# Gate steps in fours behind whole tree levels and in the attention; meta-token products over 128 rows; values turned two stages later

## The chip, the core and the metric

The kernel runs on one core of a Trainium2 chip. The metric is the device time of one execution in microseconds; of several runs the median is given. Inputs are float32. Matrix products of weights are made in three products of fp32r halves (high and low parts); the small products of the attention and of the recurrences are plain float32, which TensorE runs in two passes, so that one product is two MATMUL instructions in the trace.

## What is computed

Two blocks follow each other over 512 tokens of width 1024. The change lies in the mixer of the second block, which runs two layers over 528 tokens (16 meta tokens ahead of the 512):

```python
for l in range(DEPTH_2):                                   # two layers
    u = rms_norm_2(h, ln_mix[l])
    (aq, ak, av, bq, bk, bv, cq, ck, cv, dq, dzf, dzb, di, dg, gz) = split_in(u @ w_in[l])
    y_a = windowed_sink_attention(aq, ak, av, attn_sink[l], bias_a)
    y_b = axial_rope_attention(rms_norm_2(bq, ...), rms_norm_2(bk, ...), bv, row, col, key_ok)
    y_c = differential_attention(cq, ck, cv, lam, bias_c, key_ok, diff_subnorm[l], lam_init)
    y_d = hgrn2_bidirectional(dq, dzf, dzb, di, dg, lb_all[0, l], lb_all[1, l], valid, hgrn_out_norm[l])
    gate = jax.nn.sigmoid(gz)                              # four gates of width 1024 per token
    merged = gate[:, :, 0] * (y_a @ w_branch[l, 0])        # ... + gate n * (branch n @ w_branch[l, n])
    h = h + merged @ w_out[l]
    u = rms_norm_2(h, ln_ffn[l])
    h = h + (jax.nn.silu(u @ w_ffn_gate[l]) * (u @ w_ffn_up[l])) @ w_ffn_down[l]
```

The gates `gz` are the largest part of the projection: 4096 columns, and nothing before the merge needs them.

## The kernel before

Activations lie with features on the partitions, 528 columns (16 meta tokens, then four tiles of 128). A weight block is 128 output features by 1024 inputs. `wget` (L310) loads it on SyncE's queue into `raw` (three buffers), casts the high half `wh` on ScalarE and forms the low half `wl` on VectorE; `mm3` (L326) then makes three products for each of eight slices of the inputs.

`mixer2(l)` (L1457) runs for l = 0 and 1. In layer 0 all 528 tokens are queries, in two pieces of 264 columns; in layer 1 only the 512, in one piece. Its parts in order:

- **The gates as filler.** `gates()` (L1472) is a generator over 32 weight blocks. One call of `next` is a *gate step*: one slice of one block, that is six products `pgz` of 264 columns in layer 0 and three of 512 in layer 1. Eight steps are a block, 256 steps a layer. `self.fill(n)` (L356) takes n steps wherever the code calls it, and `self.fill(256)` after the attention takes what is left.
- **The recurrence** (`hgrn`, L1265). After ten weight blocks there are two *trees* (m = 0, 1), each for two heads, which lie on partitions 0 to 63 and 64 to 127. A tree has nine levels H = 1 to 256 and one more product of the same kind. A level forms `KH` and `QH` from `q`, the gates and running products (`QH` and the updates of `df` on VectorE, `KH` and the updates of `Sx` and `Px` on GpSimd). `put` (L1331) then multiplies them: four blocks b of 128 tokens, each for both heads, which is a *group* of four 64-row MATMUL instructions (`pA`). The result is copied into `AD` under a mask (L1348, VectorE; the first level by ScalarE). In layer 0 some levels have 16x16 products of the meta tokens as well (`pAm`). Level 128 and level 256 are copied to `A1`, `A2`, `A3` by ScalarE, the product with the meta keys to `AM` (16 rows). Then for each head x and token tile t five output products go into `pod`: four over 128 rows and one over the 16 rows of `AM` and `Vd[4]`.
- **The projections** of the other three branches: twelve weight blocks in `staged(12, first, sums, roped)`. In `staged`, stage j works on block i - j, so `sums` is one block behind `first`, and `roped` two. Blocks 3, 7 and 11 are values: `values` turns them with `turnV`, five transposes (`pvt`) that ScalarE copies into `V`. Queries and keys go to DRAM (`qkd`).
- **The third branch** (differential attention, four heads with 5 or 4 query tiles): `prepare` reads keys and queries back (`T<-qkd`, two buffers; cast to `A` on ScalarE, corrected on GpSimd), then `scores` (`pS`), `combine`, `turn` (`ptp`, transposed into `PT` for 512 keys and `PT4` for the 16 meta keys) and `product` (`po`, five products a tile, the last over 16 rows).
- **The first two branches** in `attention` (L763): eight units, each with `att_max` (`pS`), `att_exp` (`pm`, `pT`) and `att_pv` (`po`).
- **The merge** (`pbr`) and the output product (`pwo`).

The program's order on an engine is not that of the code alone: a scheduler places an instruction earlier where its operands are ready and buffers are free. Each engine then runs its list strictly in order. PSUM has eight banks: four for projections and gates (`acc`), four for everything else (`mx`).

## Time and profile before

| | |
|---|---|
| median of 3 runs | 3375.02 us (3368.74 to 3382.93) |
| profiled execution | 3379.54 us |
| its span, first to last instruction | 3377.7 us |
| mean granted TensorE clock | 0.964 of full speed |
| TensorE (PE) busy | 3262.8 us, 97% |
| VectorE (DVE) busy | 1722.3 us, 51% |
| ScalarE (ACT) busy | 1144.0 us, 34% |
| GpSimd (POOL) busy | 468.5 us, 14% |

The profiled execution's own time is 1.8 us above its span. Busy time counts an engine from the start of an instruction to its end; matmuls overlap in the array, so neighbouring starts tell more of TensorE than its busy share. In a timeline row stand the start and the time of a merged group of instructions, engine, line, operation, output<-inputs, shape and count, and in brackets the idle time before it with what ended it. Lines L241, L247, L266 and L269 are helpers that record every product, elementwise operation, activation and copy, so tiles are told apart by names. The first tree of layer 0 lies at 1317 to 1386 us of the span, its second at 1418 to 1483; those of layer 1 at 2415 to 2469 and 2498 to 2558.

### The profile page before, as it was taken

How to read it: one execution, taken by the hardware profiler on the slowest of the kernel's cores; microseconds unless marked ns; L12 is line 12 of the kernel's file. 1: busy time of each engine (PE TensorE's matmuls, PEld its weight loads, DVE VectorE, ACT ScalarE, POOL GpSimd, SP SyncE). 2: the span in 40 equal slices, each digit the busy share in tenths (PEclk: the TensorE clock that was granted, in tenths of full speed). 3: DMA queues.
4: the chain of work that ended last, by engine and by line, in shares of the span. 5: the costliest groups of instructions: out<-in, count | busy, mean ns of one | idle time of the engine just before them, and what ended most of it. 6: DMA issues, size and time to landing. Idle time of an engine off the chain costs nothing. (4 is left out here: it accounts for less than half of the span.)

```text
span 3377.7 us, 47662 instructions
## 1 busy us (share of the span) xinstructions
PE 3262.8 (97%) x18886; PEld 2770.6 (82%) x18886; DVE 1722.3 (51%) x3632; ACT 1144.0 (34%) x1958; POOL 468.5 (14%) x575
## 2 busy tenths in 40 slices
PE   8999999899999999998999999999999899999998
PEld 6778778877888889888888999999767788788886
DVE  4443378553544445654763744433665474654433
ACT  4222343366322333222642232222222453232221
POOL 1010010412000013322120300000331221400000
PEclk9999989898999999998997999999999898899999
DMA  4333213322323233233332522233223342522322
GB/s 128 104 107 115 87 63 107 99 88 69 94 94 94 94 100 110 77 102 106 108 115 68 157 88 91 93 99 116 88 84 103 117 130 88 162 90 97 93 93 77
DMA packets 121271, 337.26 MB, mean 100 GB/s; under 512 B 28853, under 2 KB 29248, under 8 KB 121048
## 3 DMA queue, kind: packets, MB, share of 16 engines
q1 hardware_dynamic: 87656, 267.95, 24.8%
q0 software_dynamic: 21712, 54.51, 5.2%
q10 hardware_dynamic: 11680, 11.76, 1.1%
q8 instruction: 148, 2.42, 0.3%
q14 instruction: 75, 0.61, 0.1%
HBM read 298.42 MB, written 39.56 MB: 100 GB/s over the span
## 5 line engine op out<-in xcount | busy, mean ns | idle before, releaser
L269 ACT CAST wh<-raw 128x1024 fp32r<-128x1024 f32 (+1 forms) x448 | 463.7, 1035 | 1571.2 <-issue 766.1
L247 DVE TENSOR_TENSOR wl<-raw,wh 128x1024 fp32r<-128x1024 f32 (+1 forms) x448 | 560.9, 1252 | 412.3 <-ACT wh L269 410.3
L241 PE MATMUL pg<-xl,wh 128*128 128x512 f32 (+1 forms) x880 | 283.2, 354 | 12.7 <-DVE xl L259 12.7
L241 PE MATMUL pg<-xh,wh 128*128 128x512 f32 (+1 forms) x880 | 282.1, 353 | 0.0
L241 PE MATMUL pu<-xl,wh 128*128 128x512 f32 (+1 forms) x880 | 281.2, 352 | 0.0
L241 PE MATMUL pd<-hl,wh 128*128 128x512 f32 (+1 forms) x880 | 281.0, 352 | 0.0
L241 PE MATMUL pu<-xh,wh 128*128 128x512 f32 (+1 forms) x880 | 280.9, 352 | 0.0
L241 PE MATMUL pd<-hh,wh 128*128 128x512 f32 (+1 forms) x880 | 280.7, 352 | 0.0
L241 PE MATMUL pg<-xh,wl 128*128 128x512 f32 (+1 forms) x880 | 280.3, 351 | 0.0
L241 PE MATMUL pu<-xh,wl 128*128 128x512 f32 (+1 forms) x880 | 279.7, 350 | 0.0
L241 PE MATMUL pd<-hh,wl 128*128 128x512 f32 (+1 forms) x880 | 278.5, 349 | 0.0
L241 PE MATMUL pgz<-xl,wh 128*128 128x264 f32 (+1 forms) x768 | 238.6, 360 | 0.0
L241 PE MATMUL pgz<-xh,wh 128*128 128x264 f32 (+1 forms) x768 | 217.8, 333 | 0.0
L241 PE MATMUL pgz<-xh,wl 128*128 128x264 f32 (+1 forms) x768 | 217.6, 332 | 0.0
L247 DVE TENSOR_TENSOR fb<-pu,rs 128x512 f32<-128x512 f32 (+1 forms) x110 | 62.6, 586 | 290.3 <-PE pu L241 290.3
L241 PEld LDWEIGHTS pg<-xl,wh 128*128 128x128 f32 x880 | 153.8, 189 | 38.2 <-DVE xl L259 14.9
L241 PEld LDWEIGHTS pu<-xh,wl 128*128 128x128 f32 x880 | 153.8, 188 | 27.3 <-issue 2.6
L241 PEld LDWEIGHTS pg<-xh,wl 128*128 128x128 f32 x880 | 154.4, 189 | 26.3 <-issue 1.7
L241 PEld LDWEIGHTS pg<-xh,wh 128*128 128x128 f32 x880 | 154.8, 189 | 25.2 <-issue 0.9
L241 PEld LDWEIGHTS pu<-xh,wh 128*128 128x128 f32 x880 | 154.1, 188 | 24.8 <-issue 0.9
L241 PEld LDWEIGHTS pd<-hh,wl 128*128 128x128 f32 x880 | 153.8, 188 | 24.9
L241 PEld LDWEIGHTS pd<-hh,wh 128*128 128x128 f32 x880 | 153.5, 188 | 24.3
(487 smaller groups left out, 6448.9 us busy)
## 6 DMA issues: line engine op xcount, KB each, us to landing
raw<-in_win SPq DMA_DIRECT2D x136, 512.0 KB
raw<-in_gu SPq DMA_DIRECT2D x88, 512.0 KB
raw<-in_f1gu SPq DMA_DIRECT2D x44, 512.0 KB
raw<-in_f2gu SPq DMA_DIRECT2D x44, 512.0 KB
raw<-in_dn SPq DMA_DIRECT2D x32, 512.0 KB
raw<-in_wout SPq DMA_DIRECT2D x24, 512.0 KB
gates<-g POOLq DMA_DIRECT2D x32, 264.0 KB, 2.7
gr<-gates SPq DMA_DIRECT2D x32, 264.0 KB
```

The lines of the kernel that those rows point to most:

```text
L241: return self.nc.tensor.matmul(out=out, lhsT=lhsT, rhs=rhs, start=start, stop=stop)
L247: return (eng or self.nc.vector).tensor_tensor(out=out, in0=a, in1=b, op=op)
L269: return self.nc.scalar.copy(out=out, in_=in_)
```

## The change

- `put` takes no gate steps between its blocks (before: 1, 2, 1, 2) but four behind all of them and behind the meta products. Level 128 takes four behind its blocks (before: one behind each), each half of level 256 three (before: one behind each of two blocks). The output products take two steps behind the fifth product instead of one behind the second and one behind the fourth. A tree therefore takes 58 steps instead of 72.
- `att_exp` takes one step ahead of its `pm` products; `product` takes its two steps behind the fifth product.
- The output products of the tree read all 128 rows of `AM` and `Vd[4]`; rows 16 to 127 are cleared by memsets on GpSimd. The same holds for `product`, with `V[4]` and two fixed tiles `T4s` in place of rotating `PT4`.
- Blocks 3, 7 and 11 are turned in `roped`, two stages behind their projection instead of one, and four gate steps are taken ahead of each. The pool `sT` has five buffers instead of four.

In all, a layer's fixed calls take 252 steps in layer 0 and 232 in layer 1, where they asked for 260 and 240; the final `fill(256)` takes the rest.

```diff
--- before.py
+++ after.py
@@ -710,6 +710,7 @@
                          ALU.subtract)
         Q1, K1, Q2, K2 = u["Q1"], u["K1"], u.get("Q2"), u.get("K2")
         QL = Q1 if Q2 is None else Q2
+        self.fill()
         for part in ((its,) if nit <= 4 else (its[4:] + its[:2], its[2:4])):
             pm = u["psum"]("pm")
             lo, hi = part[0][0], part[-1][0] + part[-1][1]
@@ -1303,6 +1304,7 @@
                 (Sb if d else P).append(f)
                 (kb if d else kf).append(k)
         Vd = [self.slab("Vd", "dV") for _ in ALL]
+        nc.gpsimd.memset(Vd[4][:, 0:256], 0.0)
         vts = [self.projV(XH, XL, ALL, "pdi", 6 + m) for m in range(2)]
         for m in range(2):
             sg = self.slab("sT", "sg")
@@ -1327,6 +1329,8 @@
             nc.gpsimd.memset(Px[:, SA], 1.0)
             AD, A1, A2, A3, AM = ([self.slab("A", n) for _ in range(2)] for n in ("AD", "A1", "A2", "A3", "AM"))
             AN = [self.small("AN", 80, bufs=2) for _ in range(2)]
+            for x in range(2):
+                nc.gpsimd.memset(AM[x][:, 0:512], 0.0)
 
             def put(i, kh, qh):
 
@@ -1335,12 +1339,12 @@
                 for b in range(4):
                     for x in range(2):
                         self.mm(pss[x][:, 128 * b:128 * b + 128], kh[rows[x], tc_[b]], qh[rows[x], tc_[b]])
-                    self.fill(2 if b % 2 else 1)
                 with_meta = l == 0 and (i < 4 or i == 7)
                 if with_meta:
                     pms = [self.mx("pAm")[:MT, :MT] for x in range(2)]
                     for x in range(2):
                         self.mm(pms[x], kh[rows[x], meta], qh[rows[x], meta])
+                self.fill(4)
                 for x in range(2):
                     if i == 0:
                         self.acopy(AD[x][:, :512], pss[x])
@@ -1382,7 +1386,7 @@
                     for b in range(4):
                         for x in range(2):
                             self.mm(pss[x][:, 128 * b:128 * b + 128], kh[rows[x], tc_[b]], qh[rows[x], tc_[b ^ 1]])
-                        self.fill()
+                    self.fill(4)
                     for x in range(2):
                         self.acopy(A1[x][:, :512], pss[x])
                     continue
@@ -1393,7 +1397,7 @@
                         for x in range(2):
                             self.mm(pss[x][:, 256 * b:256 * b + 256], kh[rows[x], tc_[2 * half + b]],
                                     qh[rows[x], o:o + 256])
-                        self.fill()
+                    self.fill(3)
                     for x in range(2):
                         self.acopy(dst[x][:, :512], pss[x])
 
@@ -1434,11 +1438,10 @@
                            (A1[x][:, 128 * (t ^ 1):128 * (t ^ 1) + 128], Vd[t ^ 1][:, hs])]
                     for b in range(2):
                         ops.append((A23[:, 256 * b + base:256 * b + base + 128], Vd[(2 if t < 2 else 0) + b][:, hs]))
-                    ops.append((AM[x][:MT, 128 * t:128 * t + 128], Vd[4][:MT, hs]))
+                    ops.append((AM[x][:, 128 * t:128 * t + 128], Vd[4][:, hs]))
                     for i, (a, b) in enumerate(ops):
                         self.mm(o, a, b, i == 0, i == len(ops) - 1)
-                        if i in (1, 3):
-                            self.fill()
+                    self.fill(2)
                 self.vcopy(y[:, :512].rearrange("p (t x) -> p t x", x=128)[:, :, 64 * x:64 * x + 64],
                            po[:, 0:256].rearrange("p (t x) -> p t x", x=64))
                 if l == 0:
@@ -1465,7 +1468,7 @@
         self.open("g", {"g": 2})
         self.open("yf", {"Y": 8})
         Y = [[self.slab("Y", "Yf") for _ in range(2)] for _ in range(4)]
-        self.open("m2", {"sT": 4, "V": 5, "rc": 2})
+        self.open("m2", {"sT": 5, "V": 5, "rc": 2})
         self.open_w(f"win2_{l}")
         gd = self.ps_dram.tile([32, 128, NC], F32, name=f"gates{l}")
 
@@ -1489,6 +1492,7 @@
 
 
         V = [self.slab("V", "V") for _ in ALL]
+        nc.gpsimd.memset(V[4][:, 0:390], 0.0)
         for t, (_, k) in enumerate(ALL):
             nc.gpsimd.memset(V[t][:k, 0:390].rearrange("p (h x) -> p h x", x=65)[:, :, 64], 1.0)
         qkd = [[self.ps_dram.tile([128, NC], F32, name="qkd") for _ in range(3)] for _ in range(3)]
@@ -1531,11 +1535,14 @@
         def sums(i, t):
             b, m, slot, scale = todo[i]
             if m == 3:
-                values(t, slot)
-            elif b == 1:
+                return t
+            if b == 1:
                 return t, self.row_scales(t, toks(m), 64, 1.0 / 64, self.acc)
 
         def roped(m, got):
+            if m % 4 == 3:
+                self.fill(4)
+                values(got, todo[m][2])
             if m > 2:
                 return
             T, y = got
@@ -1581,6 +1588,9 @@
 
         nit = len(its)
         heads = {}
+        T4s = [self.slab("u", "PT4") for _ in range(2)]
+        for t in T4s:
+            nc.gpsimd.memset(t[:, 0:128], 0.0)
 
         def prepare(h):
             p, x = divmod(h, 2)
@@ -1630,7 +1640,7 @@
 
         def turn(i, P):
             ni = its[i % nit][1]
-            T, T4 = self.slab("p", "PT"), self.slab("u", "PT4")
+            T, T4 = self.slab("p", "PT"), T4s[i % 2]
             pt = self.mx("ptp")
             pt4 = self.mx("ptp") if ni == 128 else pt[:, 448:512]
             for j, (j0, nj) in enumerate(ALL):
@@ -1647,11 +1657,10 @@
             u, ni = heads[h], its[t][1]
             y4, ym = u["y"]
             po = self.mx("po")
-            V_ = vs(4 + p)
+            z = slice(65 * (4 + p), 65 * (4 + p) + 64)
             for j in range(5):
-                self.mm(po[:ni, :64], T[:, ni * j:ni * j + ni] if j < 4 else T4[:MT, :ni], V_(j)[:, :64], j == 0, j == 4)
-                if j in (1, 3):
-                    self.fill()
+                self.mm(po[:ni, :64], T[:, ni * j:ni * j + ni] if j < 4 else T4[:, :ni], V[j][:, z], j == 0, j == 4)
+            self.fill(2)
             o = (y4[:, t] if ni == 128 else ym)[:, 64 * x:64 * x + 64]
             self.act(o, po[:ni, :64], AF.Copy, scale=u["rec"][:ni, 2 * t:2 * t + 1])
             if t == nit - 1 and x:
```

On TensorE's list, in one of the levels of the first tree of layer 0 (`pgz` are the gate products, `pA` those of the level), stands before:

```order
L241 MATMUL pA<-QH,KH 128x128 x2
L241 MATMUL pgz<-xl,wh 128x264 x2
L241 MATMUL pgz<-xh,wl 128x264 x2
L241 MATMUL pgz<-xh,wh 128x264 x2
L241 MATMUL pA<-QH,KH 128x128 x2
L241 MATMUL pgz<-xl,wh 128x264 x2
L241 MATMUL pgz<-xh,wl 128x264 x2
L241 MATMUL pgz<-xh,wh 128x264 x2
L241 MATMUL pgz<-xl,wh 128x264 x2
L241 MATMUL pgz<-xh,wl 128x264 x2
L241 MATMUL pgz<-xh,wh 128x264 x2
```

and after:

```order
L241 MATMUL pA<-QH,KH 128x128 x8
L241 MATMUL pgz<-xl,wh 128x264 x2
L241 MATMUL pgz<-xh,wl 128x264 x2
L241 MATMUL pgz<-xh,wh 128x264 x2
L241 MATMUL pgz<-xl,wh 128x264 x2
L241 MATMUL pgz<-xh,wl 128x264 x2
L241 MATMUL pgz<-xh,wh 128x264 x2
L241 MATMUL pgz<-xl,wh 128x264 x2
L241 MATMUL pgz<-xh,wl 128x264 x2
L241 MATMUL pgz<-xh,wh 128x264 x2
```

The eight products of a level stand together, with gate steps only behind them. Counted over both layers, the 128-column `pA` products stand in 138 unbroken runs before and in 37 after.

On TensorE's list at the output products of the same tree stands before, for one head and one tile:

```order
L241 MATMUL pod<-dV,AD 128x64
L241 MATMUL pod<-dV,A_10057 128x64
L241 MATMUL pgz<-xl,wh 128x264 x2
L241 MATMUL pgz<-xh,wl 128x264 x2
L241 MATMUL pgz<-xh,wh 128x264 x2
L241 MATMUL pod<-dV,A_10061 128x64 x2
L241 MATMUL pgz<-xl,wh 128x264 x2
L241 MATMUL pgz<-xh,wl 128x264 x2
L241 MATMUL pgz<-xh,wh 128x264 x2
L241 MATMUL pod<-dV,AM 128x64
```

and after:

```order
L241 MATMUL pod<-dV,AD 128x64
L241 MATMUL pod<-dV,A_10058 128x64
L241 MATMUL pod<-dV,A_10062 128x64 x2
L241 MATMUL pod<-dV,AM 128x64
L241 MATMUL pgz<-xl,wh 128x264 x2
L241 MATMUL pgz<-xh,wl 128x264 x2
L241 MATMUL pgz<-xh,wh 128x264 x2
L241 MATMUL pgz<-xl,wh 128x264 x2
L241 MATMUL pgz<-xh,wl 128x264 x2
L241 MATMUL pgz<-xh,wh 128x264 x2
```

The five products of a tile stand together. On ScalarE's list, in the projections of layer 0 (`A<-T` are the casts of keys and queries that come back from DRAM, `V` the copies of turned values, `wh` the casts of weights), stands before:

```order
L269 COPY vt<-pv 128x264
L269 CAST A_12905<-T 96x528
L269 CAST A_12910<-T 96x528
L269 CAST wh<-raw 128x1024
L266 ACTIVATE V<-pvt,ny_9308 128x2x64
L266 ACTIVATE V<-pvt,ny_9308 16x2x64
L269 CAST A_12917<-T 96x528
L266 ACTIVATE V<-pvt,ny_9308 128x2x64
L269 CAST A_12922<-T 96x528
L266 ACTIVATE V<-pvt,ny_9308 128x2x64 x2
```

and after:

```order
L269 CAST A_12793<-T 96x528
L269 CAST A_12798<-T 96x528
L269 CAST wh<-raw 128x1024
L269 CAST A_12805<-T 96x528
L269 CAST A_12810<-T 96x528
L269 CAST A_12836<-T 96x528
L269 CAST wh<-raw 128x1024
L269 CAST A_12841<-T 96x528
L269 CAST A_13096<-T 96x528
L266 ACTIVATE V<-pvt,ny_9308 128x2x64
L266 ACTIVATE V<-pvt,ny_9308 16x2x64
L266 ACTIVATE V<-pvt,ny_9308 128x2x64 x3
```

The second group of `V` copies stood from behind the second cast on, between later ones; now it stands together behind the seventh.

## Rows read from the trace of the kernel before

**Rows 1.** The page: the span, and TensorE's busy time with its weight loads

```profile
span 3377.7 us, 47662 instructions
...
PE 3262.8 (97%) x18886; PEld 2770.6 (82%) x18886; DVE 1722.3 (51%) x3632; ACT 1144.0 (34%) x1958; POOL 468.5 (14%) x575
```

**Rows 2.** Table by stretch (length; busy by engine; clock; DMA share, GB/s)

```profile
1317.00:1386.00 69.00, 69.00 (x521) 56.35 (x519) 45.53 (x79) 17.44 (x30) 27.96 (x38) 1.00 0.25 78
...
1808.00:1900.00 92.00, 82.50 (x538) 75.17 (x537) 45.28 (x93) 21.77 (x47) 27.03 (x20) 0.81 0.43 128
...
2415.00:2469.00 54.00, 54.00 (x273) 33.44 (x274) 37.11 (x54) 11.20 (x17) 23.23 (x35) 1.00 0.26 88
```

**Rows 3.** Timeline of TensorE, one tree level of layer 0

```profile
1340.43 0.49 PE L241 MATMUL pA<-QH,KH 64*128 64x128 f32 x4
...
1342.51 0.49 PE L241 MATMUL pA<-QH,KH 64*128 64x128 f32 x4
1342.93 0.51 PE L241 MATMUL pgz<-xl,wh 128*128 128x264 f32 x2
...
1343.86 0.49 PE L241 MATMUL pA<-QH,KH 64*128 64x128 f32 x4
```

**Rows 4.** The same timeline at the head of the second tree

```profile
1418.80 1.16 PE L241 MATMUL pA<-QH,KH 64*128 64x128 f32 x16
1419.89 0.22 PE L241 MATMUL pAm<-QH,KH 64*16 64x16 f32 x4
```

**Rows 5.** Timeline of VectorE over one tree level

```profile
1351.38 1.37 DVE L1348 COPY_PREDICATED AD<-hm,pA 128x512 f32<-128x512 uint32 x2
1352.65 1.37 DVE L247 TENSOR_TENSOR QH<-dq,df 128x256 f32<-128x256 f32 x2
1353.94 1.18 DVE L247 TENSOR_TENSOR df<-df 128x256 f32<-128x256 f32 x2
1355.61 0.77 DVE L247 TENSOR_TENSOR g<-pgz,rs 128x264 f32<-128x264 f32 x2 [0.50 <-PE pgz L241]
1356.86 1.23 DVE L247 TENSOR_TENSOR wl<-raw,wh 128x1024 fp32r<-128x1024 f32 x1 [0.47 <-ACT wh L269]
```

**Rows 6.** Timeline of TensorE at the output products of the first tree

```profile
1388.51 0.55 PE L241 MATMUL pod<-dV,A 128*128 128x64 f32 x4
1388.88 0.49 PE L241 MATMUL pgz<-xl,wh 128*128 128x264 f32 x2
...
1389.78 0.43 PE L241 MATMUL pod<-dV,AM 16*128 16x64 f32 x2
...
1392.69 0.43 PE L241 MATMUL pod<-dV,AM 16*128 16x64 f32 x2
```

**Rows 7.** The same timeline in the third branch's attention

```profile
1624.19 1.36 PE L241 MATMUL po<-V,PT 128*128 128x64 f32 x10
1625.48 0.53 PE L241 MATMUL pS<-A,A 96*16 96x264 f32 x3
```

**Rows 8.** Waits of TensorE in layer 0's mixer (us in total, times, longest)

```profile
PE pvt L244 <- ACT vt L269: 7.8, 1, 7.8
...
PE pvt L244 <- ACT V L266: 6.3, 4, 2.2
```

**Rows 9.** Waits of TensorE in layer 1's mixer

```profile
PE pvt L244 <- ACT vt L269: 6.5, 1, 6.5
PE pvt L244 <- ACT V L266: 5.9, 3, 2.5
```

**Rows 10.** Timeline of ScalarE: first and tenth cast of a returned key or query

```profile
1572.61 0.63 ACT L269 CAST A<-T 96x528 fp32r<-96x528 f32 x1 [2.37 <-DMA T<-qkd]
...
1609.74 0.63 ACT L269 CAST A<-T 96x528 fp32r<-96x528 f32 x1 [3.30 <-DMA T<-qkd]
```

**Rows 11.** Timeline of TensorE in the tail of layer 0's attention

```profile
1813.91 7.45 PE L241 MATMUL po<-V,P 128*128 128x65 f32 x50
...
1829.00 20.15 PE L241 MATMUL po<-V,P 128*128 128x65 f32 x100
```

## The prediction

> **What bounds the kernel now.** I read the page's first part first: TensorE is busy for 97% of a span of 3377.7 us [rows 1], so time goes away only where TensorE does less or waits less. Next the table by stretch: the change lies in the two second-block mixers, and in their tree stretches TensorE has no idle time worth naming at a granted clock of 1.00, while VectorE is busy for 45.53 of 69 us and GpSimd for 27.96 [rows 2]. "Busy" hides that TensorE pays for changing its form of work. The timeline of one tree level shows it: after each group of four 64-row instructions (`pA`, one block of 128 tokens for two heads, two passes each) come one or two gate steps of six 128-row products (`pgz`). From one group to the next it is 1.35 us with one gate step (1342.51 to 1343.86) and 2.08 us with two (1340.43 to 1342.51) [rows 3]. So a gate step costs 2.08 - 1.35 = 0.73 us, and a group 1.35 - 0.73 = 0.62 us. Of that 0.62 the group itself takes 0.42 (1342.51 to 1342.93) [rows 3]; 0.20 is the first and last 128-row product beside it being late. Where the same `pA` instructions stand sixteen in a row, once, they take 1.09 us (1418.80 to 1419.89) [rows 4], not 4 x 0.42 = 1.68.
>
> **The tree levels (gate steps behind whole levels).** A level has four groups. Before: 4 x 0.62 + 6 x 0.73 = 6.86 us. After: one run of 1.09 + 0.20 and four steps of 0.73, so 4.21 us. Two steps, 1.46 us, are only done elsewhere; 4 x 0.62 - 1.29 = 1.19 us are gone for good, 0.40 for each group joined to another. In the order of TensorE's instructions the 128-column `pA` stand in 138 runs before and in 37 after: 101 x 0.40 = **40 us**. The 256-column ones of the last level go from 16 runs to 8; the trace has none of these joined, so I price them as the others, 8 x 0.40 = **3 us** (nothing to 6). The second mixer's gate products are 512 wide, but a group ends and begins with the same two changes of form, so I use one price for both.
>
> Who is late next? VectorE, per level: two predicated copies 1.37, two `QH` products 1.37, two `df` updates 1.18, so 3.92 us, and for half a gate block (0.77 + 1.23)/2 = 1.00: 4.92 us [rows 5] against TensorE's new 4.21. It falls 0.71 us behind per level. But in the order it forms `QH` two levels ahead, the first level is copied by ScalarE, and the levels of 128 and 256 need no predicated copy (2.55 + 1.0 to 1.5 us). Stepping through the seven levels by these durations, TensorE waits about 0.4 to 1 us a tree where the meta tokens take two more PSUM buffers. I charge **4 us** for four trees; with no lead at all it would be 7 x 0.71 x 4 = 20 us. GpSimd, 27.96 us busy of 69 [rows 2], has room in a tree of some 47 us even with the new memsets: two clears of AM at the head of a tree, not waited for before the output products.
>
> **The output products (`pod`).** Before, from one 16-row product to the next it is 2.91 us (1389.78 to 1392.69) [rows 6], of which two gate steps are 1.46: 1.45 us for five products cut in two places and with a 16-row form in them. Four 128-row instructions take 0.37 us to the next start (1388.51 to 1388.88) [rows 6], so ten in one run, as now, some 0.93 to 1.1. I take 0.35 saved, 32 times: **11 us**.
>
> **The attention products (`po`, third branch).** The order had these in runs of ten already; only the padding acts. A run of eight 128-row and two 16-row instructions takes 1.29 us to the next start (1624.19 to 1625.48) [rows 7]; ten 128-row ones 0.93 to 1.1. I take 0.23, 32 times: **7 us**. The memsets that clear T4, V and Vd go to GpSimd ahead of the loops and hold up nobody.
>
> A rule speaks against this padding: the Trainium skill, "TensorEngine Tiling (Array Packing)", section Performance Considerations, says a contraction of 32 rows or fewer should take a quarter of the array's rows so that four products share it. By it the padding buys nothing, and the sum would be some 14 us smaller. In this kernel no second 16-row product stands beside the first on other rows, and the trace shows the 16-row pair as the slow one; I keep the rows.
>
> **Values turned two stages later.** TensorE waits for `pvt` 7.8 + 6.3 us in the first mixer [rows 8] and 6.5 + 5.9 in the second [rows 9]: 26.5 us, which looks like the prize of this edit. It is not TensorE's order that makes them. ScalarE is in order, and its `V` and `vt` copies stand among ten casts `A<-T`, each waiting for a copy of keys or queries from DRAM through two buffers; the first starts at 1572.61, the tenth at 1609.74, one every 4.1 us [rows 10]. After the change all ten still stand ahead of the last `vt`, and the second group of `V` copies stands behind the seventh cast, where it stood from the second on. So TensorE meets the same clock of 4.1 us: I work out one wait of about 13 us at the third `pvt` of that group and 3 to 5 us before the last value block, whose weight cast stands behind the ninth cast. In that time it does 48 more gate products (5.8 us), and the stretch ends some 5 us later. Net **0**; from a loss of 10 us over both layers (the clock falling in the long wait) to the full 26 us.
>
> **The moved steps and the tail.** Of 28 steps a layer that leave the trees, 12 go into the values, 8 into the attention (one ahead of each `pm`), the rest behind the last unit. At full clock they cost what they cost in the tree, so they are neutral except where TensorE would have waited or run slow. That is the first mixer's tail: its gate steps run out before the last units; two units' `po` run as 100 instructions in 20.15 us, where 50 took 7.45 [rows 11], in a stretch with a granted clock of 0.81 and 82.50 of 92 us busy [rows 2]. Two times 7.45 is 14.9, so 5 us are lost there alone. Now gate steps stand between the last `po`. I take **6 us** gained (0 to 14).
>
> **Sum.** 40 + 3 + 11 + 7 - 4 + 0 + 6 = 63 us. It is made on an execution of 3379.5 us (span 3377.7), 0.1% above the median of 3375.0; taken from the median, 3312 us.
>
> **Rivals.** *The turn pays after all:* if the casts no longer stand in the way, up to 26.5 us of waits go, some 24 with the copies that stay: 3288. For it: the waits are real. Against: the order of ScalarE. *VectorE binds the trees:* 20 us of waits in place of 4: 3328. For it: 4.92 against 4.21. Against: its lead of two levels. *The joined groups are not cheaper:* the run of sixteen was seen once between transposes and meta products; if half of the 61 us is bound to something else, 3342. Against: it is the same form, operands and buffers, and the change of order is there. *Slower:* the four trees lose their clock. There TensorE's gate products come in pieces of 2.9 us with `pA` and a VectorE wait between them. If those waits recur in each level and the granted clock drops to 1.2 GHz, each of 42 steps in a tree costs 0.73 us more: 42 x 0.73 x 4 = 123 us, 3435 if throughout. It eats the gain from half of the trees' time on, and makes the kernel slower by 0.5% from two thirds on. Against: these stretches hold 1.00 now, with a larger part of their time in narrow groups.
>
> **How the numbers follow.** Forecast 3312 (3302 to 3322): 0.50. The turn pays: 0.13. VectorE binds: 0.20. Groups not cheaper: 0.12, of which half would be read as no change. Slower: 0.05. The range takes the first three whole with the bounds of tail and turn, 3280 to 3345, and leaves about 0.15 outside. About 0.5%, some 17 us, is what a measurement of this kernel can tell from no change: faster 0.89, same 0.06, slower 0.05.
>
> **What would show it.** Right: in the trees' timeline `pA` in runs of sixteen of 1.09 us with four gate steps behind, levels every 4.2 to 4.4 us, a tree in some 47 to 50 us in place of 69; no 16-row `pod` or third-branch `po`; one long `pvt` wait of 10 us or more a layer on ScalarE's `V`. Wrong: `pA` waits on VectorE of over 1 us a level; a granted clock under 0.95 in the trees; `pvt` waits all but gone, which would put the time under 3300.

## The result, and the profile after

| | before | after |
|---|---|---|
| median, us | 3374.4 of 4 runs (3368.74 to 3382.93) | 3323.43 of 4 runs (3322.48 to 3325.39) |
| ratio, 95% interval | 1 | 0.9855 [0.9837, 0.9874] |
| profiled span, us | 3377.7 | 3319.7 |
| mean granted clock | 0.964 | 0.967 |

The kernel is faster by 1.45%, 51 us by the medians and 58 us by the two spans. The page after, against [rows 1]: TensorE runs as many matmuls, and is busy for 65.7 us less.

```profile
span 3319.7 us, 47744 instructions
...
PE 3197.1 (96%) x18886; PEld 2756.0 (83%) x18886; DVE 1724.0 (52%) x3632; ACT 1144.9 (34%) x1958; POOL 478.9 (14%) x591
```

The table by stretch of the kernel after (columns as in [rows 2]): the trees of layer 0, its projections and values, its plain attention, then the trees and the values of layer 1.

```profile
1317.20:1367.30 50.10, 48.65 (x457) 43.60 (x456) 43.27 (x77) 16.13 (x29) 29.21 (x40) 1.00 0.26 75
1394.80:1444.10 49.30, 45.16 (x421) 40.47 (x420) 38.47 (x72) 13.27 (x22) 24.77 (x33) 0.97 0.25 82
1466.40:1586.20 119.80, 100.86 (x751) 97.05 (x751) 49.79 (x147) 34.42 (x63) 25.05 (x25) 0.90 0.37 114
1691.10:1876.10 185.00, 180.91 (x1250) 165.15 (x1250) 108.33 (x273) 63.74 (x144) 52.83 (x44) 0.90 0.39 126
2371.80:2418.40 46.60, 45.40 (x295) 33.55 (x294) 41.06 (x59) 14.50 (x24) 28.48 (x39) 1.00 0.29 80
2444.20:2489.20 45.00, 41.77 (x274) 31.07 (x273) 38.50 (x56) 12.50 (x18) 23.65 (x33) 0.96 0.26 84
2507.80:2622.50 114.70, 100.26 (x564) 86.03 (x564) 48.36 (x115) 33.33 (x59) 26.32 (x28) 0.91 0.41 125
```

A stretch is also shorter because gate steps left it, and they come back elsewhere. To see what is gone for good, the lengths have to be corrected for the gate products in them: one costs 0.73 / 6 = 0.1215 us in layer 0, by the price of the prediction, and 0.235 us in layer 1, where four follow each other in 0.94 us:

```profile
2440.18 0.40 PE L241 MATMUL pgz<-xl,wh 128*128 128x512 f32 x1
...
2441.12 0.39 PE L241 MATMUL pgz<-xh,wl 128*128 128x512 f32 x1
```

With the gate products counted in either trace, "net" is the length lost less the price of the products that left:

| stretch (both layers) | length before, us | after, us | gate products | net gain | predicted |
|---|---|---|---|---|---|
| first trees | 70.8 and 66.7 | 50.1 and 46.6 | 337 to 252, 168 to 126 | 10.4 + 10.2 | four trees: |
| second trees | 63.8 and 58.0 | 49.3 and 45.0 | 292 to 219, 143 to 109 | 5.6 + 5.0 | 43 - 4 = 39 |
| output products `pod` | 57.5 and 52.4 | 49.8 and 44.4 | 235 to 225, 121 to 107 | 6.5 + 4.7 | 11 |
| projections and values | 111.5 and 107.7 | 125.1 and 120.0 | 48 to 123, 26 to 71 | -4.5 - 1.7 | 0 |
| third branch | 104.6 and 89.3 | 99.6 and 83.1 | 425 to 427, 189 to 190 | 5.2 + 6.4 | 7 |
| plain attention, to the last `pbr` | 183.3 and 160.1 | 185.0 and 169.4 | 200 to 290, 121 to 165 | 9.2 + 1.0 | 6 |

The sum is 58 us, that of the spans; the other stages agree within about 1 us each. The prices are those of full clock; in a stretch with a lower clock a gate product costs more, so its net figure is rougher.

**A tree level** stands in TensorE's timeline as it was forecast: one run of sixteen, four gate steps, 4.20 us from level to level (1340.66 to 1344.86) against 4.21 worked out from [rows 3, 4].

```profile
1340.66 1.16 PE L241 MATMUL pA<-QH,KH 64*128 64x128 f32 x16
1341.75 0.51 PE L241 MATMUL pgz<-xl,wh 128*128 128x264 f32 x2
...
1344.86 1.16 PE L241 MATMUL pA<-QH,KH 64*128 64x128 f32 x16
```

**The products over 128 rows**, against [rows 6, 7]: from one set of `pod` to the next it is 2.58 us (2.91 before), and a `po` run of ten gives way to `pS` after 1.03 us (1.29 before).

```profile
1369.94 0.33 PE L241 MATMUL pod<-dV,AD 128*128 128x64 f32 x2
...
1372.52 0.33 PE L241 MATMUL pod<-dV,AD 128*128 128x64 f32 x2
...
1595.50 1.23 PE L241 MATMUL po<-V,PT 128*128 128x64 f32 x10
1596.53 0.55 PE L241 MATMUL pS<-A,A 96*16 96x264 f32 x3
```

**The wait at the head of the second trees** is new. TensorE waits 4.0 us for VectorE at 1404.02, and 2.8 us at the same place in layer 1. The timeline of layer 0 (TensorE, VectorE, GpSimd) shows VectorE in one `wl` for 3.49 us, where [rows 5] have 1.23, while GpSimd runs three products. The kernel before has such a `wl` too, of 3.95 us beside the same three products, at 1389.08 (last line); but there TensorE is in the output products of the first tree and does not wait. In layer 1 the `wl` ahead of the wait takes 1.20 us, and TensorE waits for `QH` (until 2454.95), so the long `wl` is a part of the wait in layer 0 alone.

```profile
1399.75 3.49 DVE L247 TENSOR_TENSOR wl<-raw,wh 128x1024 fp32r<-128x1024 f32 x1
1400.08 0.75 POOL L247 TENSOR_TENSOR KH<-dk,Sx 128x264 f32<-128x264 f32 x1
...
1401.47 0.68 POOL L247 TENSOR_TENSOR Sx<-Sx,df 128x264 f32<-128x264 f32 x1
...
1404.02 1.28 PE L241 MATMUL pA<-QH,KH 64*128 64x128 f32 x16 [4.00 <-DVE AN L1361]
```

```profile
1389.08 3.95 DVE L247 TENSOR_TENSOR wl<-raw,wh 128x1024 fp32r<-128x1024 f32 x1
```

Over the four trees TensorE is idle for 10.0 us (length less busy time in the table by stretch: 1.45, 4.14, 1.20 and 3.23).

**The waits of the value stretches** (us in total, times, longest; layer 0, then layer 1), against [rows 8, 9]:

```profile
PE pvt L244 <- ACT V L266: 14.7, 1, 14.7
PE pss L241 <- ACT sq L266: 1.4, 1, 1.4
PE pn L241 <- ACT yxm L269: 1.1, 1, 1.1
...
PE pqk L241 <- ACT wh L269: 7.4, 2, 6.7
PE pvt L244 <- ACT V L266: 3.4, 2, 2.4
```

### The profile page after: what moved, and what is told of

Its sections match the earlier page's. It is cut to its first block, busy times and chain, and to the rows that moved or that the text cites. A ratio compares the mean times of both kernels' runs of the same rounds, so it can differ in the third digit from the quotient of the medians.

```text
span 3319.7 us, 47744 instructions
## 1 busy us (share of the span) xinstructions
PE 3197.1 (96%) x18886; PEld 2756.0 (83%) x18886; DVE 1724.0 (52%) x3632; ACT 1144.9 (34%) x1958; POOL 478.9 (14%) x591
## 3 DMA queue, kind: packets, MB, share of 16 engines
q1 hardware_dynamic: 87656, 267.95, 25.5%
## 5 line engine op out<-in xcount | busy, mean ns | idle before, releaser
L247 DVE TENSOR_TENSOR wl<-raw,wh 128x1024 fp32r<-128x1024 f32 (+1 forms) x448 | 553.8, 1237 | 405.8 <-ACT wh L269 404.7
L241 PE MATMUL pgz<-xl,wh 128*128 128x264 f32 (+1 forms) x768 | 226.4, 345 | 1.5 <-ACT vt L269 1.2
```

The costliest lines, as they stand in the source:

```text
L241: return self.nc.tensor.matmul(out=out, lhsT=lhsT, rhs=rhs, start=start, stop=stop)
L247: return (eng or self.nc.vector).tensor_tensor(out=out, in0=a, in1=b, op=op)
```

## The experiments

### The gate steps alone

```diff
--- the kernel before: only the gate steps behind whole levels
-                    self.fill(2 if b % 2 else 1)
+                self.fill(4)
...
-                        self.fill()
+                    self.fill(4)
...
-                        self.fill()
+                    self.fill(3)
```

> The kernel before with one part of the change alone: gate steps in fours behind whole tree levels (threes behind the halves of level 256); output products, attention, padding and values as before. Theory (joining 64-row groups takes away changes of form, 0.40 us per joined group): 101 x 0.40 + 3 us, less some 9 us of new waits, so the four trees lose about 33 us beyond the gate steps that leave them; with some 5 to 9 us in the first layer's tail, 3332 to 3342 us beside 3374 for the kernel before. Rival (the trees only hand work on, and the gain of the whole change is padding and tail): within 10 us of the kernel before.

Measured: 3350.8 us, ratio 0.9943 [0.9924, 0.9963], span 3352.2, 25.5 us under the kernel before. The trees are as short as in the kernel after (by stretch: first and second tree of layer 0; then the value stretch, of this kernel and of the one before):

```profile
1318.70:1368.80 50.10, 48.61 (x457) 43.56 (x456) 43.23 (x77) 16.09 (x29) 29.23 (x40) 1.00 0.27 75
1400.50:1446.80 46.30, 43.61 (x407) 39.01 (x406) 34.92 (x70) 11.62 (x20) 25.40 (x33) 0.96 0.26 87
1472.50:1590.00 117.50, 100.32 (x698) 96.65 (x698) 49.29 (x152) 32.62 (x61) 25.05 (x24) 0.85 0.36 111
```

```profile
1508.60:1615.10 106.50, 90.93 (x670) 87.50 (x670) 47.49 (x150) 30.99 (x59) 26.37 (x27) 0.89 0.41 126
```

Net, the four trees give 31.5 us, so that step of the sum holds by itself. But the value stretches lose 10.1 us net (8.0 and 2.1), though the values are turned where they were. In layer 0 TensorE now waits 1.4 us for `sq` and 1.1 us for `yxm` behind the trees, which it does not do in the kernel before, and the granted clock of the stretch is 0.85 where it was 0.89. Neither theory had this: some 10 of the 31 us are given back in the next stage. Nor did the 5 to 9 us in layer 0's tail come: its plain attention loses 1.7 us net, with no gate product between the last `pm` and the last `po`, where the kernel after has 36. So the time lies above the theory's 3332 to 3342 us, and the tail's gain seems to hang on the step that `att_exp` takes.

### Sixteen rows again

```diff
--- the kernel after
-                    ops.append((AM[x][:, 128 * t:128 * t + 128], Vd[4][:, hs]))
+                    ops.append((AM[x][:MT, 128 * t:128 * t + 128], Vd[4][:MT, hs]))
...
-                self.mm(po[:ni, :64], T[:, ni * j:ni * j + ni] if j < 4 else T4[:, :ni], V[j][:, z], j == 0, j == 4)
+                self.mm(po[:ni, :64], T[:, ni * j:ni * j + ni] if j < 4 else T4[:MT, :ni], V[j][:ALL[j][1], z], j == 0, j == 4)
```

> The changed kernel with the products of the meta tokens over 16 rows again (the memsets stay). Theory (a 16-row form between 128-row forms costs its two changes): the output products of a tree lose 7 us and those of the third branch 7 to 11, so 14 to 18 us slower than the changed kernel, 3337 to 3342 us. Rival (the Trainium skill, TensorEngine Tiling (Array Packing), Performance Considerations, on small contractions): no slower than the changed kernel, 3323 us or less.

Measured: 3342.3 us, ratio 0.9921 [0.9904, 0.9939], span 3339.4. The padding is worth what was thought: from one set of `pod` to the next it is 2.85 us again, with the runs joined as in the kernel after.

```profile
1366.51 0.33 PE L241 MATMUL pod<-dV,AD 128*128 128x64 f32 x2
...
1369.36 0.33 PE L241 MATMUL pod<-dV,AD 128*128 128x64 f32 x2
...
1597.73 1.36 PE L241 MATMUL po<-V,PT 128*128 128x64 f32 x10
1599.03 0.54 PE L241 MATMUL pS<-A,A 96*16 96x264 f32 x3
```

So 0.27 of the 0.33 us a set are the padding, 32 x 0.27 = 8.6 us, and the third branch gives another 32 x 0.27 = 8.6. The 2 to 3 us left over of the 19.7 between the spans are less than two profiles of one kernel differ by (below). The rival did not come: a single small contraction among 128-row products costs more than a padded one. The Trainium skill, "TensorEngine Tiling (Array Packing)", section Performance Considerations, would put four such small contractions beside each other; that no run here tried. Its section Key Properties says that a change of tiling mode drains the engine, and the runs fit that, with a price of 0.27 us for a 16-row pair here.

### Values turned as before

```diff
--- the kernel after
-        self.open("m2", {"sT": 5, "V": 5, "rc": 2})
+        self.open("m2", {"sT": 4, "V": 5, "rc": 2})
...
             if m == 3:
-                return t
+                values(t, slot)
...
-            if m % 4 == 3:
-                self.fill(4)
-                values(got, todo[m][2])
```

> The changed kernel with the values turned one stage after their projection as before, no gate steps ahead of them, and four sT buffers. Theory (ScalarE's casts of returned keys and queries set the pace of that stretch, so the later turn gains nothing and costs some 6 us by the trace): 3315 to 3325 us. Rival (the later turn is worth the pvt waits of the kernel before, some 24 us): 3340 us or more.

Measured: 3329.0 us, ratio 0.9888 [0.986, 0.9917], span 3326.2: 6.5 us over the kernel after by the spans, 11 by the ratios, with intervals that overlap. TensorE has the two waits of before again (layer 0):

```profile
PE pvt L244 <- ACT vt L269: 7.5, 1, 7.5
PE pvt L244 <- ACT V L266: 6.0, 4, 2.4
```

Net, the value stretches lose 8.8 us against the kernel before, as they do with the gate steps alone. So the 6.2 us that they lose in the kernel after are not the late turn's: by itself it wins 2.6 us there. One wait of 14.7 us stands for 13.5 us in five. The time lies between the two theories: the late turn does not cost 6 us, and it is not worth 24. Most of the 6.5 us between the spans lies in the plain attention of layer 1 (5.9 us net, at a granted clock of 0.86 against 0.89), far from the edit; whether the turn causes that is not shown.

### Four buffers for the loads that the casts wait for

```diff
--- the kernel after
-        self.open("at", {"T": 2, "qs": 6, "ks": 4, "p": 10, "y": 2, "u": 2})
+        self.open("at", {"T": 4, "qs": 6, "ks": 4, "p": 10, "y": 2, "u": 2})
```

> The changed kernel with four buffers T for the returned keys and queries instead of two. Theory (two buffers set the pace of 4.1 us a cast, and the casts hold the V copies on ScalarE): casts come every 2 to 2.5 us, the pvt wait of 14.7 us in the first layer falls below 8, and the kernel takes 3303 to 3315 us. Rival (the DRAM reads themselves set the pace): casts still every 4 us, the same waits, 3320 to 3326 us.

Measured: 3336.97 us, ratio 0.9901 [0.9882, 0.9921], span 3327.6: not faster, and by the ratio slower than the kernel after. ScalarE's timeline, first and tenth cast and the `V` copies:

```profile
1535.72 0.63 ACT L269 CAST A<-T 96x528 fp32r<-96x528 f32 x1 [2.93 <-DMA T<-qkd]
...
1564.16 0.63 ACT L269 CAST A<-T 96x528 fp32r<-96x528 f32 x1 [2.42 <-DMA T<-qkd]
1564.70 0.60 ACT L266 ACTIVATE V<-pvt,ny 128x128 f32<-128x128 f32 x2
```

The casts do come faster, 28.44 / 9 = 3.2 us apart in place of 4.1, though not every 2 to 2.5 us. But with buffers free the scheduler puts all ten ahead of `V`, where seven stood, and `V` comes at 1564.7, no earlier. TensorE still waits 12.3 us for it. The run changed the order as well as the pace, and so could not tell the theories apart; the next one leaves the order alone.

### The casts on GpSimd

```diff
--- the kernel after, in stack3
-        self.acopy(A[0:96, s], T[0:96, s])
+        self.nc.gpsimd.tensor_copy(out=A[0:96, s], in_=T[0:96, s])
```

> The changed kernel with one line different: the cast of a stacked key or query block, A<-T, runs on GpSimd and no longer on ScalarE. TensorE's order is the same; on ScalarE the value copies V<-pvt of the second group no longer stand behind seven casts that each wait for a load of T, and in layer 1 the weight casts wh<-raw don't either. Theory (the 14.7 us that TensorE waits for V in layer 0, the 7.4 us for wh and 3.4 us for V in layer 1, and the half clock of 23.9 and 20.5 us around them, all come from that queue on ScalarE): the stretch from the last pod to the last pv falls from 114.5 to 95-102 us in layer 0 and from 109.3 to 98-104 us in layer 1, the span from 3319.7 to 3295-3308 us, ratio to before 0.978-0.982. Rival (the stretch is held up by the loads or by VectorE, and ScalarE's queue only passes it on): TensorE waits about as long for something else, the two stretches stay within 3 us of 114.5 and 109.3, the span within 6 us of 3319.7, ratio 0.984-0.987. A second rival: the slower casts on GpSimd come late for the scores pS, a new wait of over 5 us stands there.

Measured: 3323.23 us, ratio 0.9852 [0.9836, 0.9867], span 3320.1: no change. By stretch, value stretch and third branch of layer 0, then of layer 1:

```profile
1462.00:1566.90 104.90, 99.77 (x752) 95.26 (x752) 50.27 (x148) 28.48 (x53) 26.53 (x29) 0.95 0.36 114
1572.20:1667.00 94.80, 81.65 (x671) 77.95 (x669) 68.50 (x282) 57.12 (x149) 20.10 (x26) 0.93 0.38 119
2507.80:2607.60 99.80, 95.11 (x564) 81.32 (x564) 49.76 (x115) 28.54 (x49) 28.50 (x30) 0.98 0.41 124
2613.60:2690.00 76.40, 68.46 (x410) 58.70 (x411) 57.12 (x205) 47.73 (x119) 19.53 (x24) 0.91 0.45 140
```

The local part of the theory is right: with TensorE's order unchanged, the value stretches fall from 119.8 to 104.9 and from 114.7 to 99.8 us, and the waits for `V` and `wh` are all but gone. So ScalarE's queue behind the casts was their cause. Yet the third branch grows from 80.2 to 94.8 and from 66.6 to 76.4 us. The new wait for `pS` is not the second rival's, since it is not a cast on GpSimd that comes late. A chain of rows shows what does in layer 0: TensorE's wait, ScalarE's cast that the `PT` copy stands behind, and SyncE's queue.

```profile
PE pS L241 <- ACT PT L269: 12.2, 1, 12.2
```

```profile
1584.56 1.04 ACT L269 CAST wh<-raw 128x1024 fp32r<-128x1024 f32 x1 [12.47 <-DMA raw<-in_win]
```

```profile
1555.63 0.45 SPq L321 DMA_DIRECT2D raw<-in_win  x1
1560.12 16.12 SPq L637 DMA_DIRECT2D T<-qkd  x5
1576.29 10.92 SPq L321 DMA_DIRECT2D raw<-in_win  x4
```

The weight loads stand in order behind five loads of `T`, each waiting for one of two buffers, so that no weight block is asked for in 20 us. The same five loads stand there in the kernel after (from 1561.3 us, for 16.0 us), but there TensorE is already waiting for `V`.

### Eight gate steps at the head of the second trees

```diff
--- the kernel after, in put
-                self.fill(4)
+                self.fill(8 if m and i < 2 else 4)
```

> The changed kernel with eight gate steps in place of four behind the first two levels of each layer's second tree; gate steps are only moved there from later places. Theory (the trees fell short of the forecast by some 8 us because at the head of the second tree TensorE runs out of gate steps while VectorE and GpSimd make the next QH and KH, 4.1 and 3.2 us of idle time and 3.4 us at half clock each): idle time in the two second trees falls from 4.1 and 3.2 us to under 1.5 us, no half clock there; the length of the tree less 0.1215 us (layer 0) and 0.2345 us (layer 1) for each gate product in it falls by 3 to 5.5 us each, and the span from 3319.7 to 3309-3316 us, ratio to before 0.982-0.985. Rival (VectorE is what the tree's head waits for whatever TensorE does in the meantime, so the wait only comes a level later): idle time stays at 3-4 us, the length less gate products within 1.5 us, and the span within 4 us of 3319.7.

Measured: 3319.41 us, ratio 0.9833 [0.982, 0.9847], span 3318.2. The second trees:

```profile
1396.20:1445.60 49.40, 49.25 (x469) 44.76 (x468) 42.20 (x75) 15.02 (x24) 24.43 (x34) 1.00 0.31 98
...
2447.40:2494.10 46.70, 46.24 (x298) 34.47 (x297) 41.64 (x58) 13.97 (x20) 24.57 (x34) 1.00 0.31 98
```

They are as long as in the kernel after within 2 us, with 48 and 24 more gate products in them: 5.7 and 3.9 us net, and the clock is back at 1.00. `wl` still takes 3.5 us; TensorE has work meanwhile. That closes the gap in the trees (31 + 9.6 against 39 forecast). So the theory is right in the trees, but the span of 3318.2 is the rival's. Of the 9.6 us about half reaches the end, 4.7 us against the kernel after on the same chip (below), and with intervals that overlap even that is not clear of noise. The 48 products are missing in the plain attention of layer 0, where 17 gate products are left between the last `pm` and the last `po` in place of 36, and from the end of the tree to the last `pwo` of layer 0 some 6 to 7 us are lost net; that the one causes the other is likely, but was not tried.

### Both, and the kernel after once more

> Both edits: casts A<-T on GpSimd, and eight gate steps behind the first two levels of the second trees. Theory: the two places are apart, so the gains add: 15-30 us under the changed kernel, span 3290-3305 us, ratio to before 0.975-0.981. Rival: what is gained in one stretch is given back by a lower granted clock or by missing gate steps in a later one, and the sum is under half of the two single gains.

> The changed kernel as it is, again, on the same chip as the three before it, so that gains of 4 to 20 us can be told from the difference of chips. Both theories expect its ratio to before within 0.983-0.988 and a span within 5 us of 3319.7 us.

Both together are the two edits above, of the casts and of the gate steps. Measured: 3315.73 us, ratio 0.9817 [0.9797, 0.9837], span 3318.6. The kernel after on the same chip: 3324.13 us, ratio 0.9847 [0.9829, 0.9865], span 3324.5; so one and the same kernel's profiles lie 4.8 us apart. Both together gain 8 us by the medians, with intervals that overlap, much less than the 15 to 30 forecast: the third branch is at 93.4 and 76.0 us as with the casts alone.

### The loads off SyncE's queue

```diff
--- the casts on GpSimd, and in stack3
-        T = self.copies(src, s, 3, tags[0])
+        T = self.copies(src, s, 3, tags[0], self.nc.gpsimd)
--- in copies, which has a new argument dma=None
-        self.nc.sync.dma_start(out=t[:n * rows, s], in_=src[:, s].unsqueeze(0).to_broadcast([n, rows, w]))
+        (dma or self.nc.sync).dma_start(out=t[:n * rows, s], in_=src[:, s].unsqueeze(0).to_broadcast([n, rows, w]))
```

> The run with the casts A<-T on GpSimd, and the loads T<-qkd that they wait for also issued by GpSimd, so that only weights raw are left on SyncE's queue there. Theory (the gain of 15 us in the value stretch of either layer was given back in the third branch because the weight loads stood on SyncE behind five loads of T that each wait for one of two buffers: no raw was issued from 1555.6 to 1576.3, and TensorE then waited 12.2 us for a pS behind a cast wh<-raw that waited 12.5 us for its load): the third branch, first to last ptp, falls back from 94.8 and 76.4 to 80-83 and 66-70 us, the value stretches stay at 93-101 us, and the span falls from 3320.1 to 3292-3303 us, ratio to before 0.976-0.981. Rival (the weights are late because 512 KB loads and VectorE's wl can't go faster there, whatever queue they stand on): the branch stays over 90 and 73 us or the value stretch grows again, span 3314-3324, ratio 0.983-0.987.

> The same with eight gate steps behind the first two levels of the second trees. Theory: the gains of the two are at places apart and add, 3-6 us under the run without them: span 3287-3299 us, ratio 0.974-0.980. Rival: the gate steps taken ahead are missing in the attention of layer 0, where the clock then falls over longer stretches, and the sum is no better than the run without them.

Measured: 3319.06 us, ratio 0.9848 [0.9824, 0.9872], span 3320.9, without the eight gate steps at the heads; 3307.02 us, ratio 0.9802 [0.9774, 0.983], span 3305.1, with them. Without them the kernel is no faster than the kernel after, which is the rival's time. In the third branch of layer 0 the wait of 12.2 us for the `PT` copy is gone, but the branch comes back only to 86.2 us, not to the forecast 80 to 83: TensorE waits 3.5 us for VectorE there, and the granted clock is 0.96. With the eight steps it takes 81.5 us at full clock; why they help there was not followed. In layer 1 it stays long in both runs (first the run without the steps, layer 0; then with them, layer 0 and layer 1):

```profile
1578.90:1665.10 86.20, 82.46 (x671) 78.59 (x670) 69.39 (x282) 56.87 (x149) 23.17 (x31) 0.96 0.37 116
...
1581.90:1663.40 81.50, 79.57 (x670) 75.72 (x669) 70.69 (x282) 56.84 (x149) 23.95 (x29) 1.00 0.38 119
...
2604.80:2682.30 77.50, 67.76 (x412) 56.73 (x411) 57.44 (x203) 47.35 (x119) 22.45 (x28) 0.93 0.39 118
```

In layer 1 the same pattern stands once more, in the run without the eight steps: TensorE waits 7.1 us for a `PT` copy, and this stands on ScalarE right behind a cast for the plain attention that waits for its load.

```profile
PE pS L241 <- ACT PT L269: 7.1, 1, 7.1
```

```profile
2639.74 0.62 ACT L269 CAST Q<-T 128x512 fp32r<-128x512 f32 x1 [5.71 <-DMA T<-qkd]
2640.27 0.58 ACT L269 COPY PT<-ptp 128x512 f32<-128x512 f32 x1
```

So in layer 0 the queue on SyncE was the cause of the wait, while in layer 1 the branch did not come back. The two runs differ by 12 us where 3 to 6 were forecast, but their intervals overlap.

### The plain attention's casts and loads too

```diff
--- the last kernel, in stackK and stackQ of the attention (K1 alike)
-        T = self.copies(src, s, 2, tags[0])
+        T = self.copies(src, s, 2, tags[0], self.nc.gpsimd if rows else None)
-        self.acopy(Q1[:, s], T[:, s])
+        (self.nc.gpsimd.tensor_copy if rows else self.nc.scalar.copy)(out=Q1[:, s], in_=T[:, s])
```

> The run with casts and loads of the stacked blocks on GpSimd and eight gate steps at the head of the second trees; now the loads T<-qkd and the casts K<-T and Q<-T of the plain attention are GpSimd's too. Theory (the wait that is left in layer 1, 7.1 us of pS for a PT copy in the third branch with 10.2 us at half clock, is the same queue on ScalarE once more: the PT copy stands behind the cast Q<-T, which waited 5.7 us for its load): the third branch of layer 1 falls from 77.5 to 67-71 us and the span from 3305.1 to 3294-3301 us, ratio to before 0.975-0.980. Rival (the block is only late on another engine: GpSimd waits for the same load, pS or the Toeplitz block bq comes late instead): the third branch of layer 1 stays over 74 us or the plain attention grows by as much, span 3302-3315, ratio 0.979-0.984.

Measured: 3310.73 us, ratio 0.981 [0.9796, 0.9824], span 3298.0; the third branch of layer 1 takes 77.0 us. The wait for `PT` is gone, and another stands there: TensorE for VectorE, and VectorE for a buffer of `g` whose store to DRAM is now queued on GpSimd behind the same casts.

```profile
PE ptp L244 <- DVE AN L1622: 4.8, 1, 4.8
```

```profile
DVE g L247 <- DMA gates<-g: 5.8, 1, 5.8
```

The rival is right in layer 1: here the late load held up each queue that its cast was put in. This kernel, the one before it and the two edits together (0.9817) can't be told apart. By the ratios this kernel and the one before it are 0.4 to 0.5% under the kernel after. For this one the intervals are apart; that of the one before it just touches the interval of the second measurement of the kernel after.

## Why the prediction came out as it did

The forecast was 3312 us, a gain of 63; measured were 3323.4 us, inside the range, some 1.4 us beyond the likeliest case's own, and nearer to the 3328 us of the rival "VectorE binds the trees" than to 3312. That the sum comes out within 5 us of the 58 between the spans is in part luck: trees and values bring 14 us less than forecast, third branch and tail 9 us more. Step by step:

- **Joined groups, 40 + 3 - 4 = 39 forecast, 31 measured.** The price of a change of form was right to 0.01 us per level. The first trees gave 20.6 us, half of the four trees' gain as forecast. The term that was mis-sized is the waiting on VectorE: 10.0 us of idle time in the four trees where I charged 4, of which 4.0 and 3.2 us are waits in the second trees, and 3.4 us at half clock in each of these. It did not come level by level, with 20 us in all, which the rival "VectorE binds the trees" needed, but at the head of the second trees: there a few gate products stand between three levels. With eight gate steps there the wait is gone, though `wl` still takes 3.5 us, so it takes the lack of gate products for the wait to show. In layer 0 `wl` takes three times as long besides; I had stepped through the levels with VectorE's durations from a place where GpSimd did not run beside `wl`, and the trace of before had one of 3.95 us at 1389.08.
- **`pod`, 11 forecast, 11.2 measured; `po` of the third branch, 7 forecast, 8.6 measured** by taking the padding out. The prediction's rival by which the padding buys nothing did not come: in both places together it is worth 17 us, where the prediction put it at some 14. The third branch gained 11.6 in all; 3.4 us at half clock in each layer are no longer there, which is most of the rest.
- **Values, 0 forecast, -6.2 measured.** In layer 0 the mechanism was forecast well: one wait, on `V`, behind the seventh cast, 14.7 us against 13; the 3 to 5 us before the last value block did not come. In layer 1 the one long wait for `V` did not come either: it is 3.4 us for `V` and 7.4 us for `wh`. The late turn itself is worth 2.6 us. What was left out is that the shorter trees leave something late behind them: `sq` and `yxm`, 2.5 us in layer 0, and a lower clock in the stretch. With the gate steps alone it is -10.1.
- **The tail, 6 forecast, 10.2 measured**, inside its bounds of 0 to 14; 9.2 of it lie in layer 0, as forecast.
- The spans then differ by 58 us. The other 7 us between 58 and 51 lie between profiles and medians: the profiled execution of before was 5.1 us above its median, that of after 0.9 us under its own.

What stays open: why `sq` and `yxm` come late behind a shorter tree was not tried, nor how the clock falls around them could be kept off.

## What to carry to other kernels

Where TensorE changes between narrow and full products, price the change and not the products: joining four groups was worth 1.2 us a level, and it came out to a hundredth of a microsecond from two spacings in one timeline. What such a step frees is kept only if the next stage has its inputs; correct each stretch for the filler that was moved, or the gain and its loss can't be told apart. Moving the user of a late load to another engine's in-order queue took the wait away in one place here and brought one in another: find the load, and see what else is queued with it.

## What the hardware showed that was not expected

A `wl` subtraction of VectorE took from 1.7 to 3.5 us wherever over 1.5 us of it ran beside elementwise products of GpSimd. Of the 448 in the trace after, 412 overlap with no elementwise instruction of GpSimd and take at most 1.23 us; all 17 that take over 1.6 us overlap with them by at least 0.8 us. Overlap alone is not enough: two that overlap by about 1 us took 1.2 us all the same. The Trainium skill, "GPSIMD Engine Reference", section 1. Specifications, says that the two engines share their way to SBUF and contend where VectorE has two SBUF inputs, as `wl` has; the trace agrees, and puts the price at up to 2.3 us for one instruction.
